# A two-block network on one core: convolution taps handed out step by step, convolution tiles evenly spaced

## The chip, the core and the metric

The kernel runs on one core of one Trainium2 chip. The metric is the device time of one execution in microseconds, the median of a few runs. The engines are TensorE (PE, with PEld for its weight loads), VectorE (DVE), ScalarE (ACT), GpSimd (POOL) and SyncE (SP), which here issues the DMAs. Each works through its own list of instructions in the order in which the program was laid out.

## The reference

Two blocks follow each other, each of two layers, on 512 tokens of width 1024. The first block also carries 256 context tokens through its first layer. Each layer of the first block has a mixer of three branches, and then a feed-forward part:

```
hl, hc = x*(1+scale)+shift, ctx*(1+scale)+shift        # per layer
zl, zc = hl @ w_in + b_in, hc @ w_in + b_in
attn   = softmax(q k^T) v                              # 8 heads, 2 key/value heads, rms norm and rotation on q, k
a, gt  = split(conv columns of z)                      # 1024 channels each
h      = depthwise_conv(a * sigmoid(gt), dw_w, dw_b)   # 31 taps along the tokens, per channel
conv_o = silu(layer_norm(h)) @ pw_w + pw_b
pool_o = (windowed means of 2, 4, 8, 16 tokens, less the token) @ pool_w * pool_scale
m      = gate0*attn + gate1*conv_o + gate2*pool_o
x      = layer_norm(alpha*x + g*(m @ w_out + b_out))
x      = layer_norm(alpha*x + g*ffn(x))                # w_up, a conv of 3 taps, silu, w_down
```

In layer 0 all of this is done for 768 tokens (512 + 256). In layer 1 the context only gives keys and values, and the rest is done for 512 tokens. The second block (latent attention and gated linear attention) isn't touched by the change.

## The kernel before

Activations lie with channels on the partitions, 8 tiles of 128 channels. Weights are loaded by `wload` in pieces of 512 KB; ScalarE rounds a piece to a high part (L183) and VectorE takes the low part (L186). Each projection (`proj`) is three matmuls for each 128 x 128 weight tile.

The mixer of the first block has an attention part and a rest. The attention part is written as eight streams of work, each a Python generator, and `steps[l]` is a string with one letter for each step: k and q are key/value and query projections with norm and rotation, t the transposes of queries, g the first gate's projections, h and i attention heads (one step for 256 query tokens), p the pooling branch with the third gate, c the convolution's input. `mixer` walks through the string and advances the stream of each letter.

A convolution tile takes two c steps in `conv_in`. The first projects 128 channels of `a` and puts them with zero pads into a buffer `gl`. The second projects the gate, multiplies (L591), and then issues the tile's 31 taps: one tensor_scalar (L597) and 30 scalar_tensor_tensor (L599) into a tile `y` (W in the profile), each over 783 columns in layer 0 and 512 in layer 1, each reading what the one before wrote. Then `y` is stored to DRAM (`yd`, L601). All taps of a tile are issued in that one step, at a priority offset of `cprio` = -1500.

What sets the order is a list scheduler: it lays out each engine's instructions by priority among those that it holds to be ready, priority being the place in the program, moved by `high_priority(offset)`. With an offset of -1500 a tap ranks behind what is issued up to 1500 places later.

Softmax of a head (`softmax`): VectorE takes the maximum (L495) and scales it (L497), ScalarE does the exponential (L499), VectorE the reciprocal (L501), ScalarE scales (L502). The probabilities are transposed on TensorE (L533) and split by ScalarE (L299) and VectorE (L300) into T tiles, with which TensorE multiplies the values (pv). L546 and L547 end a head's step.

After the last step comes the rest: the eight `yd` tiles are loaded (L725), column sums on TensorE (st) give mean and variance (`ln`), with L263 subtracting the mean and L738 scaling; meanwhile TensorE does the second gate's eight projections, and then the pointwise projection of the convolution (conv_pw).

Of the kernel before, what the change touches and what calls it, by code (L numbers as in the profile page):

```python
# [15 lines left out]
ALU = mybir.AluOpType  # L16
# [61 lines left out]
class Net:  # L78
# [2 lines left out]
    NC1, NT1, NW1, NU1, NP1, NB1 = 27, 11, 4, 5, 3, 30  # L81
    NC2, NCG, NCM, NG2 = 20, 13, 25, 7
    NWR, NWH = 3, 4
    wprio, cprio = 300, -1500
    wshare_attn, wshare_rest, wshare = 0, 0, 0
    nfirst = (1, 3)
    nrings = (dict(T=12, N="T", Q="T", W=5, U="W", E="X", P="A", KV="A", H="A"),
              dict(T=11, N="T", Q="T", W=4, U=5, E="X", P=3, KV=4, H="A"))
    steps = ("cckkkkggqqqthhhccqqiqiccippppppgtghhhcicqqqiicckkkkpppptppgghhccqqhqcciiippppppggthhchciiipppppp",
             "kkkkqqccggthhccqqiiccppppppggthhccqqiikkkkccppppppggthhccqqiiccppppppggthhcciipppppp")  # L90


    steps2 = "00" + "g0g1g" + "01g0" + "0100" + "cccc" + "1rlm" + "g1g1g1g1" + "v1"
# [478 lines left out]
    def conv_in(self, l, t, hs, segs, yd):  # L572

        nc, tc = self.nc, self.tc
        w = self.wload(self.a["w_in"][l, CH_AG + t], KT, 256)
        n = sum(s[1] for s in segs)
        pa = self.ps("pp")
        self.proj(pa, w, 0, P, hs, segs)
        offs, tot = self.padded(segs, 15)
        gl = self.U()  # L580
        self.zero_pads(gl, segs, offs, tot)
        for o, (c0, sn) in zip(offs, segs):
            nc.scalar.activation(gl[:, o:o + sn], pa[:, c0:c0 + sn], AF.Identity, bias=self.col(l, "b_a")[:, t:t + 1])
        yield
        pg = self.ps("pp")
        self.proj(pg, w, P, 2 * P, hs, segs)
        th = self.al("E")
        nc.scalar.activation(th[:, :n], pg[:, :n], AF.Tanh, bias=self.hbg[:, t:t + 1], scale=0.5)
        for o, (c0, sn) in zip(offs, segs):
            g = gl[:, o:o + sn]  # L590
            nc.vector.scalar_tensor_tensor(g, th[:, c0:c0 + sn], 1.0, g, ALU.add, ALU.mult)  # L591

        with tc.high_priority(offset=self.cprio):
            no = tot - 30
            y = self.al("W")[:, :no]
            ws = self.cw[:, t * 31:(t + 1) * 31]
            nc.vector.tensor_scalar(y, gl[:, 0:no], ws[:, 0:1], self.col(l, "dw_b")[:, t:t + 1], op0=ALU.mult, op1=ALU.add)  # L597
            for i in range(1, 31):
                nc.vector.scalar_tensor_tensor(y, gl[:, i:i + no], ws[:, i:i + 1], y, ALU.mult, ALU.add)  # L599
            for o, (c0, sn) in zip(offs, segs):  # L600
                nc.sync.dma_start(yd[t][:, c0:c0 + sn], y[:, o - 15:o - 15 + sn])  # L601
        yield

    def padded(self, segs, pad):

        offs, o = [], pad
        for _, sn in segs:
            offs.append(o)
            o += sn + pad
        return offs, o  # L610
# [66 lines left out]
    def mixer(self, l, xsrc, hs, toks, region):  # L677

        nc, tc = self.nc, self.tc
        last = l == DEPTH - 1  # L680
        segs = [(0, SEQ)] if last else [(0, SEQ), (SEQ, CTX)]
        ntp = 2 if last else 3
        n = SEQ if last else NTOK
# [7 lines left out]
        yd = [self.dr.tile([P, NTOK], F32, name=self.nm("yd")) for _ in range(KT)]  # L691
# [3 lines left out]
        o = {}  # L695
# [19 lines left out]
            "c": chain(self.conv_in(l, t, hs, segs, yd) for t in range(KT)),  # L715
            "p": chain(self.pool_branch(l, g, hs, segs, o, md) for g in range(4)),
        }
        for step in self.steps[l].replace(" ", ""):
            next(streams[step])
        region(2)  # L720
        self.wshare = self.wshare_rest
        ys = []
        for t in range(KT):
            y = self.B()
# [11 lines left out]
        for t in range(KT):  # L736
            y = ys[t]
# [9 lines left out]
        for pr in range(4):  # L747
            ths = gates[pr]
            w = self.wload(self.a["conv_pw"][l, pr], KT, 256)
            for i in range(2):  # L750
                c = 2 * pr + i
                ps = self.ps("pp")
                self.proj(ps, w, i * P, (i + 1) * P, vs, segs)
                o = self.B()
# [1004 lines left out]
```

## Time and profile before

| what | value |
|---|---|
| median of 3 runs | 3402.8 us (3402.74 to 3403.55) |
| the profiled execution | 3398.06 us, its span 3396.3 us |
| granted TensorE clock, mean of the span | 0.962 |
| PE busy | 3189.1 us, 94% of the span |
| PEld busy | 2663.2 us, 78% |
| DVE busy | 2134.7 us, 63% |
| ACT busy | 1414.4 us, 42% |
| POOL busy | 413.2 us, 12% |

The profile is of one execution. Busy times are sums over the span, which runs through stages with different limits, so the stretches of the two attention parts are read by themselves. Matmuls are pipelined, and a PE that is busy for all of a stretch is not at its peak for that. Behind a wait the profile names the instruction that ended it.

### The profile page before, as it was taken

The numbers are of one execution on the slowest core, as the hardware profiler recorded it, in microseconds if no ns is written. First come the engines' busy times: TensorE is split into PE (matmuls) and PEld (weight loads), VectorE is DVE, ScalarE is ACT, GpSimd is POOL, SyncE is SP. The second block draws the span as 40 slices with busy tenths as digits, with TensorE's granted clock in tenths as the row PEclk, the third lists the DMA queues.
The fourth block names the chain that finished last, engine by engine and source line by source line (L and its number), as shares of the span: only waits on it lengthen the run. The fifth ranks groups of instructions, "written<-read, shape, count | busy, mean of one in ns | idle before, by whom it ended". The sixth has DMA issues, their size and how long they took to land. (4 is left out here: it accounts for less than half of the span.)

```text
span 3396.3 us, 46629 instructions
## 1 busy us (share of the span) xinstructions
PE 3189.1 (94%) x18622; PEld 2663.2 (78%) x18622; DVE 2134.7 (63%) x3158; ACT 1414.4 (42%) x2406; POOL 413.2 (12%) x489
## 2 busy tenths in 40 slices
PE   7999999999999999998999989899998898998898
PEld 4887887878778888887888867888887666996677
DVE  6795968744554444446997966755556655666555
ACT  3444343444432122224444445532346435564464
POOL 2130322201000000002112311000001200122001
PEclk8999998999999999998999999999998998999999
DMA  6232312133333432232222233433243232442323
GB/s 254 70 125 84 122 58 69 60 118 101 100 118 132 141 119 63 60 109 88 72 70 91 78 121 113 150 98 99 88 126 110 88 99 70 156 155 80 99 91 119
DMA packets 112808, 353.45 MB, mean 104 GB/s; under 512 B 13328, under 2 KB 20048, under 8 KB 107472
## 3 DMA queue, kind: packets, MB, share of 16 engines
q1 hardware_dynamic: 112592, 350.48, 32.1%
q8 instruction: 146, 2.39, 0.3%
q14 instruction: 70, 0.57, 0.1%
HBM read 327.10 MB, written 21.23 MB: 103 GB/s over the span
## 5 line engine op out<-in xcount | busy, mean ns | idle before, releaser
L186 DVE TENSOR_TENSOR wl<-wr,wh 128x1024 fp32r<-128x1024 f32 (+1 forms) x482 | 582.7, 1211 | 354.8 <-ACT wh L183 350.2
L183 ACT CAST wh<-wr 128x1024 fp32r<-128x1024 f32 (+1 forms) x482 | 490.8, 1020 | 739.3 <-PE pp L191 692.7
L191 PE MATMUL pp<-A,wh 128*128 128x512 f32 (+1 forms) x3392 | 779.8, 345 | 14.5 <-DVE A L296 5.2
L191 PE MATMUL pp<-C,wh 128*128 128x512 f32 (+1 forms) x2328 | 650.6, 366 | 27.5 <-DVE M L1548 11.0
L191 PEld LDWEIGHTS pp<-A,wh 128*128 128x128 f32 x3392 | 537.1, 190 | 127.3 <-issue 19.7
L191 PEld LDWEIGHTS pp<-C,wh 128*128 128x128 f32 x2328 | 414.8, 192 | 111.3 <-DVE M L1548 12.7
L191 PE MATMUL pp<-A,wl 128*128 128x512 f32 (+1 forms) x1696 | 463.2, 342 | 0.0
L191 PE MATMUL pp<-C,wl 128*128 128x512 f32 (+1 forms) x1164 | 421.3, 363 | 0.0
L191 PE MATMUL pp<-B,wh 128*128 128x512 f32 (+1 forms) x1296 | 316.7, 351 | 0.1
L191 PE MATMUL pp<-M,wh 128*128 128x256 f32 (+1 forms) x1280 | 294.3, 325 | 14.5 <-ACT M L1132 7.1
L191 PEld LDWEIGHTS pp<-A,wl 128*128 128x128 f32 x1696 | 272.6, 190 | 41.5 <-issue 1.9
L599 DVE SCALAR_TENSOR_TENSOR W<-W,cw,W 128x783 f32<-128x783 f32 x240 | 275.5, 1152 | 2.6
L191 PEld LDWEIGHTS pp<-C,wl 128*128 128x128 f32 x1164 | 222.3, 191 | 36.6 <-issue 1.1
L191 PEld LDWEIGHTS pp<-M,wh 128*128 128x128 f32 x1280 | 217.2, 196 | 42.4 <-issue 10.4
L191 PEld LDWEIGHTS pp<-B,wh 128*128 128x128 f32 x1296 | 212.3, 188 | 38.4 <-issue 2.1
L211 POOL TENSOR_TENSOR s<-s,nhalf 128x2 f32<-128x2 f32 (+4 forms) x40 | 54.4, 1360 | 1433.7 <-DVE s L277 1416.4
L191 PE MATMUL pp<-M,wl 128*128 128x256 f32 (+1 forms) x640 | 204.8, 321 | 0.0
L599 DVE SCALAR_TENSOR_TENSOR W<-U,cw,W 128x512 f32<-128x512 f32 x240 | 192.8, 804 | 3.5
L191 PE MATMUL pp<-B,wl 128*128 128x512 f32 (+1 forms) x648 | 194.0, 351 | 0.0
L886 DVE SCALAR_TENSOR_TENSOR B<-pp,cols,B 128x511 f32<-128x511 f32 x66 | 43.4, 658 | 214.7 <-ACT B L883 214.7
L851 DVE SCALAR_TENSOR_TENSOR X<-pp,g,X 128x512 f32<-128x512 f32 (+1 forms) x128 | 77.0, 631 | 146.9 <-PE pp L191 146.6
L883 ACT ACTIVATE B<-pp,cols 128x768 f32<-128x768 f32 (+1 forms) x44 | 38.9, 885 | 231.0 <-PE pp L191 231.0
(402 smaller groups left out, 4753.8 us busy)
## 6 DMA issues: line engine op xcount, KB each, us to landing
wr<-w_in SPq DMA_DIRECT2D x184, 512.0 KB, 3.8
wr<-w_up SPq DMA_DIRECT2D x96, 512.0 KB, 3.8
wa<-w_ada SPq DMA_DIRECT2D x40, 1024.0 KB, 5.0
wr<-w_out SPq DMA_DIRECT2D x64, 512.0 KB, 3.9
wr<-w_down SPq DMA_DIRECT2D x48, 512.0 KB, 3.6
wr<-w_ple_gate SPq DMA_DIRECT2D x32, 512.0 KB, 3.9
Z<-w_ada SPq DMA_DIRECT2D x16, 512.0 KB, 8.4
wr<-conv_pw SPq DMA_DIRECT2D x16, 512.0 KB, 3.8
```

Of the source, the lines that this page charges most:

```text
L183: nc.scalar.copy(hi[:, :n], raw[:, :n])
L186: eng.tensor_tensor(lo[:, :n], raw[:, :n], hi[:, :n].bitcast(F32), ALU.subtract)
L191: return self.nc.tensor.matmul(out, l, r, start=start, stop=stop)
L211: self.nc.gpsimd.tensor_tensor(y, x, self.nhalf[:, :n], ALU.pow)
L599: nc.vector.scalar_tensor_tensor(y, gl[:, i:i + no], ws[:, i:i + 1], y, ALU.mult, ALU.add)
L851: nc.vector.scalar_tensor_tensor(xs[t][:, c0:c0 + sn], ps[:, c0:c0 + sn], g5[:, t, q:q + 1], xs[t][:, c0:c0 + sn], ALU.mult, ALU.add)
L883: nc.scalar.activation(y[:, :n], pa[:, :n], AF.Identity, bias=self.col(l, "fdw_b")[:, f:f + 1], scale=cw[:, 1:2])
L886: nc.vector.scalar_tensor_tensor(y[:, c0 + 1:e], pa[:, c0:e - 1], cw[:, 0:1], y[:, c0 + 1:e], ALU.mult, ALU.add)
```

## The change

Three things change in the first block. The string `steps` of each layer has its c pairs at other places; the order of all other letters stays. Pairs then start every 12 steps in layer 0 and every 9 or 10 in layer 1, where they started 6 to 17 steps apart. `conv_in` no longer issues its taps but puts them into a list, and `mixer` issues some of them after each step, so many that the list is empty when the next pair begins: 2 to 4 a step. And `cprio` is 0, so that a tap ranks by its place in the program. The store of a tile is issued with its last tap.

```
-    wprio, cprio = 300, -1500
+    wprio, cprio = 300, 0
-    steps = ("cckkkkggqqqthhhccqqiqiccippppppgtghhhcicqqqiicckkkkpppptppgghhccqqhqcciiippppppggthhchciiipppppp",
-             "kkkkqqccggthhccqqiiccppppppggthhccqqiikkkkccppppppggthhccqqiiccppppppggthhcciipppppp")
+    steps = ("cckkkkggqqqtcchhhqqiqiipccpppppgtghhcchiqqqiikkkcckpppptppggcchhqqhqiiipccpppppggthhcchiiipppppp",
+             "kkkkqqccggthhqqiccippppppgccgthhqqiicckkkkpppccpppggthhccqqiippppccppggthhiccipppppp")
...
+        self.taps += [(tap, i) for i in range(31)]
         yield
+
+    def some_taps(self, n):
+
+        with self.tc.high_priority(offset=self.cprio):
+            for tap, i in self.taps[:n]:
+                tap(i)
+        del self.taps[:n]
...
-        for step in self.steps[l].replace(" ", ""):
+
+        steps = self.steps[l]
+        cs = [i for i, x in enumerate(steps) if x == "c"]
+        starts = cs[0::2] + [len(steps)]
+        self.taps = []
+        for i, step in enumerate(steps):
+            if i in starts:
+                self.some_taps(len(self.taps))
             next(streams[step])
+            if self.taps:
+                left = min(x for x in starts if x > i) - i
+                self.some_taps(-(-len(self.taps) // left))
+        self.some_taps(len(self.taps))
```

Three places in the resulting order. The first is VectorE's list in layer 0 at the end of the second convolution tile (its `y` is W_1427 before and W_1216 in the change); W_1956 is the third tile's `y`. s are softmax scalars, T probabilities or normed queries, wl the low parts of weights. Before:

```order
L591 SCALAR_TENSOR_TENSOR W_1897<-X_1952,W_1897 128x256
L300 TENSOR_TENSOR T_1787<-pt_1781,T_1786 128x512
L501 RECIPROCAL s_2001<-s_1999 128x1
L599 SCALAR_TENSOR_TENSOR W_1427<-W_1368,cw_310,W_1427 128x783
L597 TENSOR_SCALAR W_1956<-W_1897,cw_310,cols_88 128x783
L599 SCALAR_TENSOR_TENSOR W_1427<-W_1368,cw_310,W_1427 128x783
L495 TENSOR_REDUCE s_2009<-ps_2004 128x1
L599 SCALAR_TENSOR_TENSOR W_1956<-W_1897,cw_310,W_1956 128x783
L497 TENSOR_TENSOR s_2011<-s_2009,s_1085 128x1
```

The change, where taps have the line numbers 599 (the first) and 601:

```order
L601 SCALAR_TENSOR_TENSOR W_1216<-W_1157,cw_310,W_1216 128x783
L186 TENSOR_TENSOR wl_1970<-wr_1968,wh_1969 128x1024
L601 SCALAR_TENSOR_TENSOR W_1216<-W_1157,cw_310,W_1216 128x783
L186 TENSOR_TENSOR wl_1976<-wr_1974,wh_1975 128x1024
L495 TENSOR_REDUCE s_1745<-ps_1737 128x1
L497 TENSOR_TENSOR s_1747<-s_1745,s_1081 128x1
L300 TENSOR_TENSOR T_1633<-pt_1627,T_1632 128x512
L501 RECIPROCAL s_1751<-s_1749 128x1
L300 TENSOR_TENSOR T_1648<-pt_1642,T_1647 128x512
L495 TENSOR_REDUCE s_1762<-ps_1754 128x1
```

Before, the third tile's first tap stands between the second tile's last two; in the change 28 other instructions stand between the two tiles.

The second place is VectorE's list at the end of layer 1's attention part. W_16889 (before) and W_16972 (the change) are the last tile's `y`; L670 and L682 are the same line of the pooling branch. Before:

```order
L300 TENSOR_TENSOR T_17046<-pt_17040,T_17045 128x512
L599 SCALAR_TENSOR_TENSOR W_16889<-U_16857,cw_13005,W_16889 128x512
L300 TENSOR_TENSOR T_17061<-pt_17055,T_17060 128x512
L599 SCALAR_TENSOR_TENSOR W_16889<-U_16857,cw_13005,W_16889 128x512 x3
L300 TENSOR_TENSOR T_17076<-pt_17070,T_17075 128x512
L599 SCALAR_TENSOR_TENSOR W_16889<-U_16857,cw_13005,W_16889 128x512 x2
L547 SCALAR_TENSOR_TENSOR X_16922<-X_16630,X_16922 128x256
L599 SCALAR_TENSOR_TENSOR W_16889<-U_16857,cw_13005,W_16889 128x512 x6
L186 TENSOR_TENSOR wl_17497<-wr_17495,wh_17496 128x1024
```

The change:

```order
L300 TENSOR_TENSOR T_17018<-pt_17012,T_17017 128x512
L300 TENSOR_TENSOR T_17033<-pt_17027,T_17032 128x512
L601 SCALAR_TENSOR_TENSOR W_16972<-U_16940,cw_13005,W_16972 128x512 x3
L300 TENSOR_TENSOR T_17048<-pt_17042,T_17047 128x512
L601 SCALAR_TENSOR_TENSOR W_16972<-U_16940,cw_13005,W_16972 128x512 x3
L547 SCALAR_TENSOR_TENSOR X_16816<-X_16614,X_16816 128x256
L601 SCALAR_TENSOR_TENSOR W_16972<-U_16940,cw_13005,W_16972 128x512 x10
L186 TENSOR_TENSOR wl_17497<-wr_17495,wh_17496 128x1024
L601 SCALAR_TENSOR_TENSOR W_16972<-U_16940,cw_13005,W_16972 128x512 x2
L186 TENSOR_TENSOR wl_17503<-wr_17501,wh_17502 128x1024
L601 SCALAR_TENSOR_TENSOR W_16972<-U_16940,cw_13005,W_16972 128x512 x7
```

The last tile starts later among the heads: behind the last head's L547 stand 19 taps and two weight splits, where 6 taps stood.

The third place is TensorE's list just behind, around the broadcast of the convolution's mean (cmean). pp_17507 and pp_17534 are gate projections, st the sums of the layer norm. Before:

```order
L191 MATMUL pp_17507<-C_12918,wh_17496 128x512
L191 MATMUL pp_17507<-C_12919,wh_17496 128x512
L191 MATMUL st_17312<-B_17310,cmean 128x512
L191 MATMUL pp_17507<-C_12918,wl_17497 128x512
L191 MATMUL pp_17507<-C_12924,wh_17502 128x512
L191 MATMUL pp_17507<-C_12925,wh_17502 128x512
```

The change:

```order
L191 MATMUL pp_17534<-C_12943,wh_17502 128x512
L191 MATMUL pp_17534<-C_12942,wl_17503 128x512
L191 MATMUL st_17312<-B_17310,cmean 128x512
L191 MATMUL st_17322<-B_17326,ones 32x512
L191 MATMUL st_17322<-B_17323,ones 32x512
L191 MATMUL st_17322<-B_17324,ones 32x512
```

Before, 34 gate matmuls stand between the broadcast and the second column sum (st_17322); in the change they have moved ahead of the broadcast.

## Rows read from the trace of the kernel before

**Rows 1.** The page's first part: busy time, share of the span, instructions.

```profile
PE 3189.1 (94%) x18622; PEld 2663.2 (78%) x18622; DVE 2134.7 (63%) x3158; ACT 1414.4 (42%) x2406; POOL 413.2 (12%) x489
```

**Rows 2.** Busy time by stretch of the two attention parts; columns in the first line.

```profile
core 0: us, PE busy (x) PEld busy (x) DVE busy (x) ACT busy (x) POOL busy (x), PEclk, DMA share, GB/s
...
140.00:170.00 30.00, 25.01 (x185) 22.57 (x185) 22.16 (x39) 14.49 (x31) 0.00 (x0) 1.00 0.06 18
170.00:250.00 80.00, 79.32 (x499) 66.41 (x498) 79.57 (x98) 35.02 (x70) 24.11 (x27) 1.00 0.36 115
295.00:325.00 30.00, 24.08 (x166) 19.76 (x164) 16.55 (x39) 19.62 (x42) 0.00 (x0) 1.00 0.11 36
325.00:426.00 101.00, 97.20 (x650) 83.49 (x649) 99.85 (x118) 34.03 (x79) 39.38 (x46) 1.00 0.36 114
475.00:577.00 102.00, 94.77 (x552) 83.13 (x551) 100.74 (x125) 42.53 (x91) 32.90 (x35) 0.92 0.16 49
625.00:690.00 65.00, 57.93 (x331) 49.76 (x330) 58.77 (x75) 29.16 (x50) 22.72 (x21) 0.92 0.27 88
...
1700.00:1785.00 85.00, 77.55 (x517) 70.76 (x516) 78.63 (x121) 39.65 (x82) 15.70 (x13) 0.96 0.22 70
...
1960.00:2003.00 43.00, 34.60 (x182) 28.32 (x181) 40.20 (x66) 22.97 (x37) 4.45 (x5) 0.92 0.30 91
```

**Rows 3.** Costliest groups (busy, mean ns, idle before), and tap durations min/median/max.

```profile
L186 DVE TENSOR_TENSOR wl<-wr,wh 128x1024 fp32r<-128x1024 f32 (+1 forms) x482 | 582.7, 1211 | 354.8 <-ACT wh L183 350.2
L599 DVE SCALAR_TENSOR_TENSOR W<-W,cw,W 128x783 f32<-128x783 f32 x240 | 275.5, 1152 | 2.6
...
L599 DVE SCALAR_TENSOR_TENSOR W<-W,cw,W x240: 1007/1032/2610, 68.1 to 671.0; 128x783 f32<-128x783 f32 x120
L599 DVE SCALAR_TENSOR_TENSOR W<-U,cw,W x240: 732/752/1831, 1601.6 to 2003.5; 128x512 f32<-128x512 f32 x120
```

**Rows 4.** Timeline around 551 us: start, duration, instruction, idle before and releaser.

```profile
551.01 0.15 DVE L497 TENSOR_TENSOR s<-s,s 128x1 f32<-128x1 f32 x1
...
551.20 0.56 ACT L499 ACTIVATE A<-ps,s,s 128x256 f32<-128x256 f32 x1 [1.65 <-DVE s L497]
...
552.41 1.01 PE L191 MATMUL pp<-A,wh 128*128 128x512 f32 x2 [2.57 <-ACT A L299]
```

**Rows 5.** Timeline around 1774 us.

```profile
1773.72 1.28 DVE L300 TENSOR_TENSOR T<-pt,T 128x512 fp32r<-128x512 f32 x2
...
1774.46 1.65 PE L191 MATMUL pv<-T,KV 128*128 128x256 f32 x6 [2.80 <-DVE T L300]
```

**Rows 6.** Timelines of VectorE and of GpSimd around 250 us.

```profile
249.80 2.61 DVE L599 SCALAR_TENSOR_TENSOR W<-W,cw,W 128x783 f32<-128x783 f32 x1
...
248.82 2.75 POOL L672 TENSOR_TENSOR X<-X,X 128x768 f32<-128x768 f32 x1 [1.78 <-DVE X L670]
```

**Rows 7.** Timelines of VectorE and TensorE behind layer 1's attention part.

```profile
1998.34 0.43 DVE L547 SCALAR_TENSOR_TENSOR X<-X,X 128x256 f32<-128x256 f32 x1
1998.69 5.60 DVE L599 SCALAR_TENSOR_TENSOR W<-U,cw,W 128x512 f32<-128x512 f32 x6
...
2026.03 4.87 DVE L263 TENSOR_TENSOR B<-B,st 128x512 f32<-128x512 f32 x8 [1.30 <-PE st L191]
...
1997.63 0.62 PE L191 MATMUL pp<-C,wh 128*128 128x512 f32 x2
...
2014.05 1.07 PE L191 MATMUL st<-B,ones 128*32 128x512 f32 x8
...
2024.97 1.02 PE L191 MATMUL st<-B,cmean 128*128 128x512 f32 x2
...
2033.85 1.06 PE L191 MATMUL st<-B,ones 128*32 128x512 f32 x8
...
2044.33 1.06 PE L191 MATMUL st<-ident,s 128*128 128x128 f32 x8
...
2056.95 2.50 PE L191 MATMUL pp<-C,wh 128*128 128x512 f32 x5 [6.18 <-ACT C L299]
```

More of the change, by code (lines that the diff above doesn't have):

```diff
@@ L591, in conv_in, with tap @@
             nc.vector.scalar_tensor_tensor(g, th[:, c0:c0 + sn], 1.0, g, ALU.add, ALU.mult)
[L593 to L598, printed above, removed]
+        no = tot - 30
+        y = self.al("W")[:, :no]
+        ws = self.cw[:, t * 31:(t + 1) * 31]
+        def tap(i):
+            if i == 0:
+                nc.vector.tensor_scalar(y, gl[:, 0:no], ws[:, 0:1], self.col(l, "dw_b")[:, t:t + 1], op0=ALU.mult, op1=ALU.add)
+            else:
                 nc.vector.scalar_tensor_tensor(y, gl[:, i:i + no], ws[:, i:i + 1], y, ALU.mult, ALU.add)
-            for o, (c0, sn) in zip(offs, segs):
-                nc.sync.dma_start(yd[t][:, c0:c0 + sn], y[:, o - 15:o - 15 + sn])
+            if i == 30:
+                for o, (c0, sn) in zip(offs, segs):
+                    nc.sync.dma_start(yd[t][:, c0:c0 + sn], y[:, o - 15:o - 15 + sn])
+        self.taps += [(tap, i) for i in range(31)]
         yield
+    def some_taps(self, n):
[3 more added lines that the diff above has]
+        del self.taps[:n]
     def padded(self, segs, pad):
```

## The prediction

> **What bounds the kernel now.** I read the page's busy times first: TensorE is busy for 94% of the span, VectorE for 63% [rows 1]. The change touches only the two attention parts of the first block (about 50 to 690 us and 1560 to 2003 us), so I cut these into stretches [rows 2]. In the PE column the reader is to see what is missing to the length of each stretch, in the DVE column whether VectorE is full, in the PEclk column the granted share of the 2.4 GHz level (the other level is 1.2 GHz). Idle time below is a stretch's length less its PE busy time; clock lost is the length times what PEclk lacks to 1. Three kinds of stretch show.
>
> Where two convolution tiles follow each other closely, VectorE is full for some 100 us: 99.85 of 101 and 100.74 of 102 us. TensorE idles 3.8 us in the first and 7.2 us in the second, where it also gets a clock of 0.92, so 0.08 x 102 = 8.2 us of full clock are not granted. The fill between 170 and 250 us costs 0.7 us.
>
> Where heads run without taps, VectorE has room (16.55 of 30 us) and TensorE idles all the same, 5.9 and 5.0 us per 30: that is the latency of a softmax.
>
> At the end of each attention part, taps and the last softmaxes share VectorE: 7.1 us idle and 5.2 us of clock in layer 0, 8.4 and 3.4 us in layer 1. The stretch 1700 to 1785 loses 7.5 and 3.4 us.
>
> How a full VectorE reaches TensorE is seen at 551 us [rows 4]: the scaling of a softmax bound (L497, 0.15 us) stands behind a weight split and a tap. ScalarE's exponential waits 1.65 us for it, the cast behind it on ScalarE is late, and TensorE, which needs that cast for a projection, waits 2.57 us. At 1774 us it is direct [rows 5]: VectorE comes to two probability splits (L300) only at 1773.72, and TensorE waits 2.80 us for them.
>
> **The change part by part.** No instruction is added or removed: 496 taps (16 tiles of 31), the same matmuls, the same DMAs. All that changes is order. A tap takes 1.032 us in layer 0 and 0.752 us in layer 1 at the median [rows 3], so a tile is some 32 or 23 us of VectorE. Two edits do the reordering, and I take them together: the scheduler no longer ranks taps below everything for 1500 steps, and the tiles' starts lie 9 to 12 steps apart, where they lay 6 to 17 apart.
>
> Counting in the two orders, layer 0 has today only two tiles (the first and last) that stand alone: the second and third run into each other, as do the fourth and fifth and the sixth and seventh. Afterwards all eight stand alone, with 8 to 30 other VectorE instructions between one tile's last tap and the next one's first. That is what should shorten the fills.
>
> Terms, with half-clock time counted as lost:
> 1. 475 to 577 us: 7.2 + 8.2 = 15.4 us lost today. Bounds 0 (the loss moves along with the taps) and -15.4 (as at 170 to 250, which lost 0.7). I take half, -8, since half of the taps remain in one fill.
> 2. 325 to 426 us: -2 of 3.8, by the same half.
> 3. 295 to 325 us: three head steps run there on end before the next convolution's matmuls; afterwards two. Bounds 0 and -5.9; I take -3.
> 4. 140 to 170 us: convolution matmuls now come before the heads, but taps come among them too. Bounds -5.0 and +5; I take -1.
> 5. 1700 to 1785 us: 10.9 us lost. Taps that stand directly ahead of a probability split fall from 51 to 29 in layer 1. I take -5, bounds 0 and -10.9.
> 6. The end of layer 1, 1960 to 2003 us: 11.8 us lost. Afterwards the last tile's taps stand behind nearly all softmaxes instead of among them. The heads then look like 295 to 325 us, which lost 20% without taps; 20% of 43 us is 8.6, so -3.
> 7. The seam behind it pays. Today six taps follow the last head's product (L547), 5.60 us, then the store, the loads and the first column sum at 2014.05 us [rows 7]. Afterwards 19 taps and two weight splits follow before the last tap is done: 13 x 0.752 + 2 x 1.21 = 12.2 us later [rows 3, 7]. Cover: TensorE has gate projections; 70 matmuls stand today between the last head's product and the column sum, 131 then. Today's 70 take 2014.05 - 1997.63 = 16.4 us, 0.235 each, so 131 take 30.7. The data would be there 0.7 + 0.43 + 14.3 + 2.4 + 9.8 = 27.6 us after the last product, 9.8 being today's way from last tap to column sum. So the later taps are hidden with 3 us to spare; if the cover is gone, each us is paid. But the gate matmuls spent there are missing later. Between the mean's broadcast at 2024.97 and the second column sum at 2033.85, 34 matmuls fill today, none then, and the eight subtractions end at 2026.03 + 4.87 = 2030.9: some 5 us of idle. Before the pointwise projection 12.6 us pass from 2044.33 to 2056.95; 27 matmuls (6.3 us) and the broadcast's 1.1 us leave 5.2 us idle, where 6.18 us were. In all +4. On the SP queue the last tile's store still stands ahead of the eight loads; the last gate and first pointwise weights have moved ahead of it, so its being late holds no weights back.
> 8. New waits among heads: taps directly ahead of a softmax's reciprocal (L501) rise from 21 to 31 in layer 0. Ten more taps are at most 10.3 us, and most meet an exponential that is still running; +4, bounds 0 and 10.
> The end of layer 0 (12.3 us lost) keeps its order nearly, and its gate projections stand as they did: 0, with bounds of 3 either way.
>
> Sum: -8 - 2 - 3 - 1 - 5 - 3 + 4 + 4 = **-14 us**. The profiled execution took 3398.1 us (1.8 around its span); less 14 is 3384.1. The three runs' median lies 4.7 above it, so 3388.8, say **3389 us**.
>
> A tap stretches when GpSimd works: 2.61 us beside an addition of 2.75 us [rows 6]. Layer 0's 240 taps take 275.5 us where 240 x 1.032 would be 247.7, so 27.8 us are stretch [rows 3]. The head stretches at 140 and 295 us, which get taps now, show no GpSimd work [rows 2]. The Trainium skill, Perfetto Trace Analysis, section Optimizing Scalar/DVE Operations, says that GpSimd's only SBUF port is one that VectorE shares. The trace agrees (2.61 against 1.032 us). By that rule taps should lie where GpSimd is idle, and half of the 27.8 us would leave VectorE's fills; by the trace that is up to 14 us of VectorE's time, of which I count none, since taps also stay beside the query and pool steps.
>
> **The rivals.** *The fills' loss goes whole.* For it: 170 to 250 us is full for 80 us and costs 0.7 us, so losses come late in a fill, and a shorter one may end before. Against: the lone last tile lost 12.3 us in 65. Terms 1, 2 and 5 would take their full 15.4, 3.8 and 10.9, terms 3, 4 and 6 as above 7, and the seam's 4 and half of term 8 come on top: -31, 3372 us.
>
> *No net change.* The scheduler already put taps into what it held to be idle VectorE time, and still does; the same work then causes the same waits elsewhere. For it: most waits are of 1 us, one tap long, and the taps stay between the same softmax links. 3403 us.
>
> *Slower, by lone tiles among heads.* Afterwards the second, fourth and sixth tile of layer 0 each share VectorE with 36 to 40 other instructions, mostly softmax. Today's lone last tile shares with 31 and costs 12.3 us. Three such cost 36.9; the five stretches that they replace cost 5.0 + 0.7 + 5.9 + 3.8 + 15.4 = 30.8. With the seam's 4 us, and layer 1 gaining nothing, that is +10: 3413 us. It decides from 30.8 / 3 = 10.3 us per tile on. Against it: at 170 us such a fill was cheap.
>
> **How the numbers follow.** Forecast 0.40, whole gain 0.15, no net change 0.23, slower 0.22. A measurement tells some 0.2%, 6.8 us, from no change. Faster by more: all of the forecast but its upper edge, and the whole gain, 0.54. Within: 0.24. Slower: the third rival, 0.22. The range runs from just under the whole gain, 3370, to the slower rival, 3413; some 2 in 10 lie outside. The forecast alone would be 3380 to 3397.
>
> **What would show it.** In the profile after, stretches of full VectorE in layer 0 should be 50 to 60 us long and not 100, and the granted clock should not fall to 0.92 over the fill that ends before 577 us today (terms 1, 2). Taps' maximum and sum show the GpSimd part. Term 5 is right if no wait of 2 to 3 us on L300 is left in layer 1. Term 7 shows as idle time of TensorE between the mean's broadcast and the second column sum, about 5 us, which does not exist today. If the first column sum waits for a load, the cover was too short. The prediction is wrong if TensorE's idle time over the six stretches of layer 0, 29.7 us today, stays what it is (no net change), or if a half-clock stretch appears in each of the tiles among heads (slower).

## The result, and the profile after

The changed kernel takes 3426.45 us at the median (3420.51 to 3426.95, four runs), the one before on the same chip 3402.77 (3402.37 to 3403.55). The ratio is 1.0070 (95%: 1.0057 to 1.0082): slower by 23.7 us. The forecast was 3389 us, in a range of 3370 to 3413. The profiled execution took 3426.95 us (span 3424.8, granted clock 0.956; before 3396.3 and 0.962).

The page's first part, answering [rows 1], in the same columns: every engine has as many instructions as before, and busy times differ by less than 1%, apart from GpSimd's (403.0 for 413.2). TensorE's grows by 18.5 us.

```profile
PE 3207.6 (94%) x18622; PEld 2674.8 (78%) x18622; DVE 2136.5 (62%) x3158; ACT 1417.5 (41%) x2406; POOL 403.0 (12%) x489
```

The stretches, answering [rows 2]: after each stretch its length, busy time and count by engine, then granted clock, DMA share and GB/s.

```profile
core 0: us, PE busy (x) PEld busy (x) DVE busy (x) ACT busy (x) POOL busy (x), PEclk, DMA share, GB/s
147.00:177.00 30.00, 21.89 (x117) 18.28 (x116) 27.78 (x44) 13.21 (x25) 0.00 (x0) 0.77 0.00 1
177.00:257.00 80.00, 79.26 (x497) 67.20 (x498) 61.63 (x82) 37.06 (x78) 18.57 (x26) 1.00 0.31 97
330.00:380.00 50.00, 44.16 (x297) 39.48 (x298) 41.42 (x56) 20.53 (x60) 14.65 (x15) 0.86 0.27 85
380.00:485.00 105.00, 104.54 (x629) 89.22 (x627) 70.34 (x88) 32.83 (x53) 23.27 (x32) 1.00 0.34 106
485.00:525.00 40.00, 33.50 (x195) 29.82 (x193) 37.55 (x52) 19.03 (x51) 8.10 (x7) 0.79 0.05 14
525.00:592.00 67.00, 66.37 (x403) 58.66 (x402) 53.82 (x67) 29.64 (x48) 20.07 (x28) 1.00 0.22 64
642.00:710.00 68.00, 56.63 (x311) 47.45 (x310) 62.71 (x82) 28.94 (x52) 20.67 (x21) 0.90 0.24 80
1722.00:1808.00 86.00, 80.04 (x519) 71.54 (x518) 79.15 (x120) 41.14 (x85) 14.05 (x13) 0.98 0.24 72
1980.00:2025.00 45.00, 36.04 (x187) 30.02 (x187) 34.57 (x56) 23.41 (x38) 3.46 (x2) 0.92 0.32 93
```

Loss is again idle time plus length times what PEclk lacks to 1. Three short stretches stand out, those of layer 0's second, fourth and sixth tile: 8.1 + 0.23 x 30 = 15.0 us, 5.8 + 7.0 = 12.8 and 6.5 + 8.4 = 14.9. The end of layer 0 (642 to 710) loses 11.4 + 6.8 = 18.2, where it lost 12.3. The long fill before 577 us, which lost 15.4, is gone as a stretch (525 to 592: 0.6).

Stretches of two kernels don't hold quite the same work, so the two traces are also laid over each other by work done: at a moment of the kernel before, how much later has the changed kernel done the same amount of matmuls (each counted with its usual duration)? Such lags are good to some 2 us. The changed kernel falls behind by 10 us at the second tile; by 10 at the fourth, of which 3 come back; by 13 at the sixth, which all come back in the rest of the fill behind it; and by 7 at layer 0's end. It is some 23 us behind at 700. Layer 1 gives 2 back, and the seam behind it takes 10.

Inside such a stretch, the timeline around 160 us (start, duration, engine, line, instruction, idle before and releaser; "..." stands for lines left out):

```profile
157.17 0.68 DVE L300 TENSOR_TENSOR T<-pt,T 128x512 fp32r<-128x512 f32 x1
157.91 0.85 PE L191 MATMUL pv<-T,A 128*128 128x256 f32 x5 [1.12 <-DVE T L300]
...
159.58 1.03 DVE L601 SCALAR_TENSOR_TENSOR W<-W,cw,W 128x783 f32<-128x783 f32 x1
...
160.53 0.15 DVE L497 TENSOR_TENSOR s<-s,s 128x1 f32<-128x1 f32 x1
160.71 0.99 ACT L499 ACTIVATE A<-ps,s,s 128x768 f32<-128x768 f32 x1 [0.89 <-DVE s L497]
...
161.34 1.44 PE L191 MATMUL pv<-T,A 128*128 128x256 f32 x5 [1.07 <-DVE T L300]
...
171.28 1.43 PE L191 MATMUL pv<-T,A 128*128 128x256 f32 x5 [1.23 <-DVE T L300]
```

One tap of 1.03 us stands ahead of most links of the softmax (a link is an operation that the next engine of the chain waits for: L497, L501, L300); TensorE, which has only heads here, waits about 1 us again and again. No single wait is long, yet the granted clock is 0.77 over the stretch, part of it at the lower level.

The taps' groups, answering [rows 3] (duration min/median/max in ns):

```profile
L601 DVE SCALAR_TENSOR_TENSOR W<-W,cw,W x240: 1010/1034/2614, 68.4 to 694.7; 128x783 f32<-128x783 f32 x120
L601 DVE SCALAR_TENSOR_TENSOR W<-U,cw,W x240: 731/752/1811, 1623.1 to 2036.2; 128x512 f32<-128x512 f32 x120
```

### The profile page after: what moved, and what is told of

Read it like the earlier page. It is cut to its first block, busy times and chain, and to the rows that moved or that the text cites. A ratio compares the mean times of both kernels' runs of the same rounds, so it can differ in the third digit from the quotient of the medians.

```text
span 3424.8 us, 46635 instructions
## 1 busy us (share of the span) xinstructions
PE 3207.6 (94%) x18622; PEld 2674.8 (78%) x18622; DVE 2136.5 (62%) x3158; ACT 1417.5 (41%) x2406; POOL 403.0 (12%) x489
## 5 line engine op out<-in xcount | busy, mean ns | idle before, releaser
L183 ACT CAST wh<-wr 128x1024 fp32r<-128x1024 f32 x482 | 490.2, 1019 | 776.1 <-PE pp L191 723.8
L186 DVE TENSOR_TENSOR wl<-wr,wh 128x1024 fp32r<-128x1024 f32 x482 | 581.5, 1209 | 363.0 <-ACT wh L183 349.7
L601 DVE SCALAR_TENSOR_TENSOR W<-W,cw,W 128x783 f32<-128x783 f32 x240 | 276.9, 1154 | 3.1
L191 PEld LDWEIGHTS pp<-M,wh 128*128 128x128 f32 x1280 | 218.2, 197 | 42.1 <-issue 10.9
```

The source lines that it names most:

```text
L183: nc.scalar.copy(hi[:, :n], raw[:, :n])
L186: eng.tensor_tensor(lo[:, :n], raw[:, :n], hi[:, :n].bitcast(F32), ALU.subtract)
L191: return self.nc.tensor.matmul(out, l, r, start=start, stop=stop)
```

## The experiments

Each run is compared with the kernel before on its own chip. The scatter of one kernel's runs is some 10 us, so ratios and their 95% intervals are used; 0.1% is 3.4 us.

### Which half of the change, which layer

The kernel before with the new rows of steps alone:

```
-    steps = ("cckkkkggqqqthhhccqqiqiccippppppgtghhhcicqqqiicckkkkpppptppgghhccqqhqcciiippppppggthhchciiipppppp",
-             "kkkkqqccggthhccqqiiccppppppggthhccqqiikkkkccppppppggthhccqqiiccppppppggthhcciipppppp")
+    steps = ("cckkkkggqqqtcchhhqqiqiipccpppppgtghhcchiqqqiikkkcckpppptppggcchhqqhqiiipccpppppggthhcchiiipppppp",
+             "kkkkqqccggthhqqiccippppppgccgthhqqiicckkkkpppccpppggthhccqqiippppccppggthhiccipppppp")
```

> The kernel before with nothing but the two new rows of steps; the taps are still handed out in one piece and still rank 1500 steps behind everything. Theory (the places of the tiles are the whole change): 3426 us, as the changed kernel. Rival (handing the taps out in small groups with rank 0 puts them ahead of the softmax links and costs the time): 3403 us, as before.

Measured: 1.0070 (1.0050 to 1.0089), the changed kernel's own ratio.

The opposite, the changed kernel with the old rows:

> The changed kernel with the two old rows of steps, so that only the handing out of taps in groups and the rank of 0 are left of the change. Theory (the places of the tiles are the whole change): 3403 us, within 4 us of before. Rival (handing out and rank cost the time): 3426 us.

Measured: 0.9997 (0.9983 to 1.0010). Handing the taps out in groups, and their rank, do nothing that can be measured here (between 6 us less and 3 more); the places of the `c` steps are the change.

The changed kernel with the old row in layer 1, then with the old row in layer 0:

> The changed kernel with the old row of steps in layer 1 and the new one in layer 0. By cumulative matmul work the changed kernel is some 23 us behind at 700 us, 3 us of which layer 1's attention gives back, and 9 us are lost at the seam behind layer 1. Theory (layer 0's tiles among heads cost most): 3403 + 23 = 3426 us less the scatter of a profile, 3420 to 3427, so that layer 0 alone makes two thirds or more of the loss. Rival (the loss is the seam's, and layer 0's 23 us in one profile are chance): 3403 to 3410 us.

> The changed kernel with the old row of steps in layer 0 and the new one in layer 1. Theory: the seam's 9 us less 3 us in layer 1's attention, 3403 + 6 = 3409 us, with 3403 to 3413 as bounds. Rival (the loss is the seam's): 3412 to 3426 us.

Measured: 1.0063 (1.0043 to 1.0083) and 1.0011 (1.0001 to 1.0020). Layer 0 makes some 21 us, layer 1 and its seam some 4, with an interval that nearly reaches nothing.

### Taps or projections

The changed kernel without most taps of the three tiles (87 of 93 are left out, so the network's result is no longer computed and only the time is of use), and the kernel before without the same ones; these two are called "few taps":

```
-        self.taps += [(tap, i) for i in range(31)]
+        few = l == 0 and t in (1, 3, 5)
+        self.taps += [(tap, i) for i in ((0, 30) if few else range(31))]
...
-            for i in range(1, 31):
+            for i in ((30,) if l == 0 and t in (1, 3, 5) else range(1, 31)):
```

> The changed kernel, but layer 0's second, fourth and sixth tile have only taps 0 and 30 of their 31 (87 taps are left out); everything else stands where the change put it. Theory (taps between the links of the softmaxes cost TensorE the time): the stretches of these three tiles lose 15.0, 12.8 and 14.9 us in the changed kernel (idle and half clock); without the taps they lose about what heads without taps lose, 5 to 6 us each, so that this kernel comes 24 to 30 us below the changed one, 3395 to 3402 us, and within 10 us of the kernel before with the same taps left out. Rival (the tiles' projections, which filled TensorE between the heads, now stand ahead of them, and that costs the time): the losses stay, the time is 3418 to 3426 us, and some 23 us lie between the two kernels with fewer taps.

> The kernel before, with the same 87 taps of layer 0's second, fourth and sixth tile left out, as the yardstick for the changed kernel without them. The long fills of 325 to 426 and 475 to 577 us lose 3.8 and 15.4 us; with the taps of one tile of two gone, 10 to 19 us of these should go: 3384 to 3393 us by the theory that full VectorE costs the time. By the rival (filler decides) nothing goes: 3400 us.

Measured: 0.9993 (0.9982 to 1.0004) and 0.9957 (0.9941 to 0.9973). The same 87 taps cost 0.77% = 26 us where the change puts them and 0.43% = 15 us where they were. 0.36% = 12 us still lie between the two without them, so these taps are not all. By work done the two differ by only 2 us over the three pairs of tiles (140 to 590 us), where the full kernels differ by 16; what is left lies at layer 0's end and at the seam, some 8 us each, less 2 in layer 1 (the table further down). So the places of these 87 taps account for nearly all that layer 0 loses before its end, and for nothing of its end.

How a link of the softmax stands without taps ahead, in the timeline of the changed kernel with few taps:

```profile
157.24 0.17 DVE L501 RECIPROCAL s<-s 128x1 f32<-128x1 f32 x1 [1.21 <-ACT A L499]
...
158.46 0.86 PE L191 MATMUL pv<-T,A 128*128 128x256 f32 x5 [0.34 <-DVE T L300]
```

VectorE waits for ScalarE here, not the other way round, and TensorE's wait here is 0.34 us, where it was 1.12.

The tiles behind their heads. The edit moves three pairs; the sixth tile's too, which the expectation doesn't name:

```
-"cckkkkggqqqtcchhhqqiqiipccpppppgtghhcchiqqqiikkkcckpppptppggcchhqqhqiiipccpppppggthhcchiiipppppp"
+"cckkkkggqqqthhhccqqiqiipccpppppgtghhhcciqqqiikkkcckpppptppgghhccqqhqiiipccpppppggthhcchiiipppppp"
```

> The changed kernel with one edit to layer 0's row of steps: the two steps of the second tile stand behind the three head steps instead of ahead of them, the fourth tile's behind one head step more. The tiles stay alone. Theory (a tile whose taps meet heads without projections costs 13 to 15 us): the second tile's loss of 15.0 us falls to 5 to 6 and its taps move to the query and key projections behind, so 3415 to 3418 us; the fourth tile, whose taps still meet the same softmaxes, keeps its loss. Rival (lone tiles cost the time wherever they stand): 3426 us.

Measured: 1.0028 (1.0017 to 1.0040), 0.42% = 14 us below the changed kernel. In the trace the second tile's loss goes, the sixth falls, the fourth stays, as was said:

```profile
140.00:170.00 30.00, 24.99 (x186) 22.56 (x184) 22.01 (x39) 14.34 (x30) 0.00 (x0) 1.00 0.07 18
330.00:380.00 50.00, 47.42 (x320) 41.98 (x321) 33.07 (x44) 19.05 (x64) 21.12 (x24) 0.89 0.38 124
485.00:525.00 40.00, 36.51 (x230) 31.71 (x229) 39.54 (x46) 16.77 (x48) 21.49 (x20) 1.00 0.10 26
```

(At the fourth tile 8.1 us are seen in this stretch; by work done it is 11 behind there, of which 3 come back.) The sixth tile's stretch at 485 us loses 3.5 us with VectorE just as full as in the changed kernel: a full VectorE does not cost TensorE time by itself.

### Can the fill's gain be had alone

The kernel before with the seventh tile behind the three head steps and the first pooling step that followed it (the expectation calls this one step later):

```
-"...gghhccqqhqcciiippppppggthhchciiipppppp"
+"...gghhccqqhqiiipccpppppggthhchciiipppppp"
```

> The kernel before with one edit to layer 0's row of steps: the two steps of the seventh tile move one step later, behind the pooling step that stood after them, as in the changed kernel; nothing else moves. In the order this parts the sixth and seventh tile, whose 62 taps fill 475 to 577 us and lose 15.4 us there. Theory (the fill's late half is what costs, and the change's gain there can be had alone): 8 to 15 us less than before, 3385 to 3395 us on a chip where before takes 3400. Rival (the loss moves along to where the seventh tile goes): 3400 us.

Measured: 0.9999 (0.9991 to 1.0007): the theory failed. The stretches of this run, whose profiled execution (3408.78 us) is 8 us above its median:

```profile
500.00:552.00 52.00, 48.67 (x291) 42.09 (x290) 45.63 (x60) 25.54 (x49) 14.56 (x18) 1.00 0.18 56
552.00:577.00 25.00, 23.59 (x138) 19.86 (x137) 24.22 (x26) 8.28 (x12) 10.46 (x14) 1.00 0.29 96
645.00:710.00 65.00, 52.91 (x288) 41.92 (x287) 43.80 (x62) 25.61 (x43) 10.53 (x9) 0.87 0.39 140
```

The fill's end is clean (1.4 us lost, clock 1.00), and by work done some 12 us are won there; 4 of them are paid ahead of it, beside the sixth tile, and 10 at layer 0's end (12.1 idle and 8.5 of clock).

Two more places: the seventh tile behind the three head steps but ahead of the pooling steps, and the eighth earlier; then four tiles beside projections:

```
-"cckkkkggqqqthhhccqqiqiccippppppgtghhhcicqqqiicckkkkpppptppgghhccqqhqcciiippppppggthhchciiipppppp"
+"cckkkkggqqqthhhccqqiqiccippppppgtghhhcicqqqiicckkkkpppptppgghhccqqhqiiiccppppppccggthhhiiipppppp"
...
+"cckkkkggqqqthhhccqqiqiccippccppppgtghhhiqccqqiikkcckkpppptppccgghhqqhqiiiccppppppggthhhiiipppppp"
```

> The kernel before with layer 0's seventh tile one step later (as in the run with one pair moved) and its eighth four steps earlier, ahead of the gates instead of between the last heads; layer 1 as before. When the seventh tile alone was moved, the fill before 577 us gave 13.4 us, the stretch at 500 to 547 us took back 5.3 and the end of layer 0 some 10. Theory (the end paid because the eighth tile's taps, starting later, met more of the last heads): with the eighth tile ahead of the heads these lose what heads without taps lose, 20% of 43 us = 8.6 instead of 12.3: 3400 - 13 + 5 - 4 = 3388 us, bounds 3380 to 3394. Rival (the loss moves along wherever the tiles go, since the last heads lack projections, not VectorE): 3397 to 3404 us.

> The kernel before with layer 0's fourth, sixth, seventh and eighth tile set so that their taps run beside query, key and pooling projections and end before the heads that follow; the second and third tile stay, the fifth moves two steps. In the order 54 taps stand directly ahead of a link of a softmax in layer 0, where the kernel before has 69 and the changed one 83. Theory (what a tap costs depends on whether it stands between the links of a softmax): the fill of 475 to 577 us gives most of its 15.4 us back and the last heads some 4, while pooling steps, beside which a tap stretches to 2.6 us, take some 4: 3385 us, bounds 3375 to 3394. Rival (the same losses turn up elsewhere): 3397 to 3406 us.

Measured: 1.0011 (0.9998 to 1.0024) and 1.0005 (0.9995 to 1.0016). Both rivals hold. Where the second run, with fewer taps ahead of links (54), still loses is seen at 320 us and at 360 us, with all instructions first, and then at 320 us with TensorE's on `pp` (the projections) alone:

```profile
320.00:340.00 20.00, 14.58 (x81) 12.19 (x79) 10.45 (x24) 12.31 (x23) 0.00 (x0) 0.86 0.01 4
360.00:380.00 20.00, 15.36 (x116) 13.98 (x115) 19.89 (x23) 4.62 (x15) 5.07 (x3) 0.92 0.29 90
...
320.00:340.00 20.00, 0.00 (x0) 0.86 0.01 4
```

At 320 us no tap is near (VectorE 10.45 of 20), no projection runs, and 5.4 us idle and 2.8 of clock are lost: heads left alone lose by themselves. But at 360 us VectorE is full again (19.89 of 20), taps stand between the last heads' probability splits, TensorE waits up to 1.23 us for one of these, and 4.6 + 1.6 us are lost.

The new row in layer 1 with the last tile's second step where it was:

```
-"...ppccggthhiccipppppp"
+"...ppccggthhcciipppppp"
```

> The kernel before with the new row of steps in layer 1, but its last tile's second step one step earlier, where it was; layer 0 as before. In the order 23 instead of 10 other VectorE instructions stand among the last tile's taps, so it ends nearer to the last head. Theory (layer 1's attention gains 3 us and the seam behind it costs, because the last tile ends late): the seam's cost goes, 3397 us where the new row as it is took 3404. Rival (the last tile's place is not what costs at the seam): 3404 us.

Measured: 1.0005 (0.9994 to 1.0015), which isn't told apart from the 1.0011 of the new row as it is. In its trace the seam costs nothing more (-1 us by work done), but the last heads cost some 3 to 5: paid before instead of behind.

### Query projections among the heads

In the changed kernel no projection runs from 150.5 to 179.9 us, as its timeline shows:

```profile
150.24 0.28 PE L191 MATMUL pp<-wh,A 128*128 128x256 f32 x1
...
178.75 0.68 DVE L394 TENSOR_TENSOR T<-pp,brow 128x512 f32<-128x512 f32 x1
...
179.88 0.28 PE L191 MATMUL pp<-wh,A 128*128 128x256 f32 x1
```

By the code `pp` has two PSUM buffers, and the results of two query projections stand in them until VectorE reads the first (L394, at 178.75 us). That this comes so late because its T buffer is held by the heads is argued from the code and not shown. Setting `q` steps between `h` steps lets them go on, in layer 0's new row (first), in the old (second), and in the old with two tiles moved (third):

```
-"cckkkkggqqqtcchhhqqiqiipccpppppgtghhcchiqqqiikkkcckpppptppggcchhqqhqiiipccpppppggthhcchiiipppppp"
+"cckkkkggqqqtcchqhqhiqiipccpppppgtghqhcchqiqiikkkcckpppptppggcchqhqhqiiipccpppppggthhcchiiipppppp"
...
-"cckkkkggqqqthhhccqqiqiccippppppgtghhhcicqqqiicckkkkpppptppgghhccqqhqcciiippppppggthhchciiipppppp"
+"cckkkkggqqqthqhccqhiqiccippppppgtghqhqhcicqiicckkkkpppptppgghqhccqhqcciiippppppggthhchciiipppppp"
+"cckkkkggqqqthqhccqhiqiccippppppgtghqhqhcicqiicckkkkpppptppgghqhqhqcciiiccppppppggthhchciiipppppp"
```

> The row of layer 0 that the change brings, with the query steps set between the head steps at three places; the convolution's steps stay ahead of the heads; layer 1 as before. In the order 90 taps stand directly ahead of a link of a softmax in layer 0; with the changed kernel's row it is 83. Theory (what costs is that no projection can run among the heads): the three tiles' losses of 15.0, 12.8 and 14.9 us fall to some 5 each, so from the 3421 us that layer 0's new row gave alone to 3393 us, bounds 3385 to 3403. Rival (taps between the links cost): 3421 us or more.

> The kernel before with the query steps of layer 0 set between the head steps at three places; the convolution's steps keep their places among the others, and as many taps as before stand ahead of softmax links (70, before 69). Theory (projections among the heads decide): the head stretches at 140 to 170 us (5.0 us lost), 295 to 325 (5.9) and 540 to 577 (some 14) lose a third of that: 3400 - 17 = 3383 us, bounds 3375 to 3391. Rival (taps decide): 3398 to 3402 us.

> As the run before it (query steps among the heads), and at the third place the sixth tile stands behind the heads h and the seventh behind the heads i, instead of among and ahead of them. Theory (projections among the heads decide; in the order the last heads of layer 0 have more projections among them than before): a further 2 to 6 us less than the run before it, 3379 us, bounds 3370 to 3389. Rival (as for the seventh tile alone: what the fill gives, the end takes): the same as the run before it.

Measured: 1.0054 (1.0040 to 1.0069), 1.0001 (0.9989 to 1.0012) and 1.0022 (1.0013 to 1.0032). The theory that projections alone decide falls: 3 of the 21 us come back in the first by the ratios, nothing in the second, and the third is slower. In the second the first two places do win, some 3 and 5 us by work done, and 8 are paid between 320 and 440 us. One of the waits there, in its timeline:

```profile
414.32 2.33 POOL L645 TENSOR_TENSOR W<-W 128x776 f32<-128x776 f32 x1 [1.31 <-DVE A L300]
415.23 2.25 DVE L599 SCALAR_TENSOR_TENSOR W<-W,cw,W 128x783 f32<-128x783 f32 x1
...
417.40 0.68 DVE L300 TENSOR_TENSOR T<-pt,T 128x512 fp32r<-128x512 f32 x1
...
418.13 0.66 PE L483 MATMUL pt<-ident,T 128*128 128x128 f32 x4 [1.99 <-DVE T L300]
```

A tap stretched to 2.25 us, beside a GpSimd addition of 2.33, holds a split that TensorE waits for. It is the split of transposed queries (L483), not of a softmax: again a tap ahead of a link, in another chain and at a new place.

### The square

Layer 0's new row with few taps, without and with query steps among the heads (the edits of above, together):

> Layer 0's new row of steps on the kernel before, layer 1 as before, with the 87 taps of layer 0's second, fourth and sixth tile left out. Both theories: the changed kernel without these taps took 3401 us, and layer 1's new row costs some 4 of it: 3397 us, bounds 3392 to 3402.

> The same with the query steps set among the head steps at three places, and the same 87 taps left out. If the two causes add up (heads without projections lose time by themselves, taps or not), the query steps take back their 7.7 us here too: 3389 us, bounds 3385 to 3393, which is where the kernel before stands without these taps. If taps cost only where no projection runs and heads lose nothing by themselves that projections can fill, the query steps bring nothing here: 3395 to 3400 us.

Measured: 0.9977 (0.9965 to 0.9989) and 0.9968 (0.9958 to 0.9978). The taps are worth 0.86% = 29 us in both pairs (1.0063 to 0.9977, 1.0054 to 0.9968), about twice what the same taps cost in the old row; the query steps 0.09% = 3 us in both, which the intervals don't tell from nothing.

The second tile's stretch, 140 to 180 us, shows both more sharply, since up to 140 us all kernels run alike (within 2 us by work done). In this order: before; changed; layer 0's new row with q among heads; few taps; few taps and q among heads; before with q among heads.

```profile
140.00:180.00 40.00, 35.01 (x256) 31.11 (x256) 32.16 (x50) 20.23 (x47) 7.86 (x6) 1.00 0.13 40
```

```profile
140.00:180.00 40.00, 31.16 (x187) 27.08 (x186) 37.60 (x59) 16.77 (x32) 0.00 (x0) 0.83 0.04 13
```

```profile
140.00:180.00 40.00, 32.63 (x215) 28.73 (x214) 38.34 (x55) 17.97 (x37) 3.50 (x3) 0.87 0.17 58
```

```profile
140.00:180.00 40.00, 34.55 (x250) 30.19 (x249) 21.92 (x44) 25.19 (x56) 6.01 (x6) 1.00 0.11 39
```

```profile
140.00:180.00 40.00, 36.32 (x261) 32.26 (x261) 21.32 (x40) 22.82 (x51) 5.49 (x6) 1.00 0.19 65
```

```profile
140.00:180.00 40.00, 38.07 (x271) 33.24 (x270) 32.90 (x49) 19.24 (x45) 7.67 (x9) 1.00 0.28 93
```

| loss in 140 to 180 us (idle + clock) | query steps behind the heads | among them |
|---|---|---|
| taps ahead of the heads (new row) | 8.8 + 6.8 = 15.6 | 7.4 + 5.2 = 12.6 |
| the same, few taps | 5.4 | 3.7 |
| taps behind the heads (before) | 5.0 | 1.9 |

Taps in front of heads cost 9 to 10 us in this stretch, projections among the heads give 2 to 3, and the two add up: with projections among the heads, taps in front of them cost about as much as without. In these 40 us 27 and 24 taps start in the dear cases (VectorE busy 37.6 and 38.3), 14 and 13 in the kernels with the old row (32.2 and 32.9), 1 in those with few taps (21.9 and 21.3). So by these rows half a tile, begun behind the first heads, costs nothing over no tile at all, and most of a tile in front of them 9 to 10 us.

## Why the prediction was wrong

**The view of the bound held.** TensorE is lost to links of softmaxes that stand behind taps, as read at 551 us [rows 4] and as the kernels with few taps show.

**The sum, stretch by stretch.** Us lost (+) or won (-) against the kernel before, by work done; "rows" is the kernel before with the new rows of steps alone, "layer 0" the changed kernel with layer 1's old row. Differences of 2 us say nothing, and the two profiled executions lie 28.9 us apart, 5 more than the medians.

| stretch of the kernel before | terms | forecast | changed | rows | layer 0 | changed, few taps | before, few taps |
|---|---|---|---|---|---|---|---|
| 140 to 250 us, second and third tile | 4 | -1 | +10 | +11 | +10 | +1 | -2 |
| 250 to 470, fourth and fifth | 2, 3 | -5 | +7 | +6 | +7 | -1 | -5 |
| 470 to 590, sixth and seventh | 1 | -8 | 0 | 0 | -2 | -9 | -4 |
| 590 to 705, end of layer 0 | | 0 | +7 | +9 | +7 | +8 | 0 |
| 1600 to 1998, layer 1 | 5, 6 | -8 | -2 | -1 | +2 | -3 | 0 |
| 1998 to 2100, seam | 7 | +4 | +10 | +8 | 0 | +8 | 0 |

Term 8's +4 was spread over layer 0's heads.

**The step that failed: terms 1, 3, 4 and 8, what a tile costs when it is set alone among heads.** The prediction took half of the long fill's loss as won (-8) and put the taps that land on heads at almost nothing (-3, -1 and +4 in all). Term 1's loss did not go: the fill's end came clean, and the sixth tile, now in front of its heads at 485 us, loses as much (14.9 for 15.4). That is the bound of 0 that term 1 itself named, "the loss moves along with the taps". Term 4 gave the heads at 140 us -1, bounded by +5; they cost +10. Term 3 counted on -3; the fourth tile there costs +10, of which 3 come back. Term 2's loss did go (380 to 485 us loses 0.5), but what it wins is small beside that. Without the 87 taps the new row loses nothing at these places.

The rows for a lone tile among heads were at hand: the last one, 12.3 us in 65 [rows 2]. The prediction used it for the rival and, for the forecast, set against it that the fill at 170 us cost 0.7. That row was the wrong neighbour: of TensorE's 79.3 busy us there 65.5 are projections, and five softmaxes run in 80 us; from 147 to 177 us of the changed kernel it is 3.5 of 21.9, and five in 30. The stretch at 140 us was also misread as one without taps: the second tile begins in its middle, and 11 taps follow up to 170 us.

```profile
154.82 0.68 DVE L597 TENSOR_SCALAR W<-W,cw,cols 128x783 f32<-128x783 f32 x1
```

**The rival "slower, by lone tiles among heads"** is what happened, with 15.0, 12.8 and 14.9 us for the 12.3 it priced and above its threshold of 10.3, and with the sign that was named for it, a half-clock stretch in each of the three tiles. It had 3413 us, +10. What it lacked up to 3426 is a tile's price (2 us more each), the 6 us that the stretches between the tiles still lose (it put them at nothing), layer 0's end (held at 0 with 3 either way; +7) and the seam; layer 1 gave a little back.

**Term 5** was a gain, by half: its stretch loses 7.7 us instead of 10.9, and the wait at 1774 us [rows 5] is gone, but one of the kind is left among the last heads, against the prediction's own sign:

```profile
2013.28 1.12 PE L191 MATMUL pv<-T,KV 128*128 128x256 f32 x6 [2.16 <-DVE T L300]
```

**Term 6** was to give 3: 1980 to 2025 us loses 9.0 + 3.6 = 12.6, where 11.8 were lost. Nothing.

**Term 7** had its mechanism right and its size wrong. The seam, answering [rows 7], in TensorE's timeline:

```profile
2059.05 1.94 PE L191 MATMUL st<-B,ones 128*32 128x512 f32 x8 [4.37 <-ACT B L242]
2061.44 1.94 PE L191 MATMUL st<-B,ones 128*32 128x512 f32 x8 [0.46 <-ACT B L242]
...
2086.60 2.50 PE L191 MATMUL pp<-C,wh 128*128 128x512 f32 x5 [5.65 <-ACT C L299]
```

The late taps are hidden and the wait ahead of the second column sum is 4.4 us (5 were said). What was left out is the clock: behind that wait the eight sums take 1.94 us where they took 1.06 [rows 7]. From the last head's product to the pointwise projection it is 9.6 us more, not 4. With layer 0 as before the same row made the seam only some 5 us dearer; why is open.

**Two edits taken together.** The prediction did not separate them; the first two runs show that only the new rows of steps do anything that can be measured.

**The stretch beside GpSimd**, counted as none, stayed: the 240 taps of layer 0 take 276.9 us in all and 240 x 1.034 = 248.2 at the median, 28.7 of stretch where it was 27.8. The Trainium skill, Perfetto Trace Analysis, section Optimizing Scalar/DVE Operations, says that GpSimd's only SBUF port is one that it shares with VectorE. The tap of 2.25 us beside GpSimd's addition at 414 us, shown above, agrees with that. Moving the tiles apart did not take taps out of GpSimd's way.

**What stays open.** Why layer 0's end pays: in all nine kernels whose seventh tile stands behind the first pooling step, it costs 7 to 10 us by work done, with the 87 taps or without. Moving the eighth tile ahead, with the seventh ahead of the pooling steps, made it 13. With the seventh there, the eighth as before and query steps among the heads the end cost nothing (-1), but the stretch of the sixth and seventh tile lost 10 instead. What takes back the 8 us that query steps win at two places of the old row is seen in one wait and not counted through. No layout tried beats the kernel before; six lie within 0.2% of it (layer 1's new row, the seventh tile moved, the eighth early, four tiles beside projections, layer 1's last pair, query steps among the heads of the old row).

## What to carry to other kernels

Price a piece of filler from a stretch that has the same neighbours. A full VectorE cost TensorE 0.7 us in 80 where softmaxes were few, and a tile of 32 us cost some 10 us where it stood in front of heads, whether or not query projections ran among them. When a full stretch is split, ask what the parts land on before counting the gain: here the 15 us that the fill gained were lost again by the tile just ahead of it, and two more landing places came on top with 10 and 7. Lay two traces over each other by work done before calling a stretch's loss won; a loss can leave one stretch and stand in the next. Where a change has two edits, find out first whether each of them changes the order at all.

## What was not expected of the hardware

The granted clock fell without any long wait. In the changed kernel it is 0.66 from 160 to 180 us, a mean over both levels (1.2 and 2.4 GHz), where TensorE's waits are 1.2 us at the longest, as they are in the 20 us before:

```profile
160.00:180.00 20.00, 14.83 (x65) 12.16 (x66) 18.47 (x32) 8.95 (x20) 0.00 (x0) 0.66 0.00 1
```

With few taps TensorE idles 3.1 us in the same 20, with some projections among the heads, and the clock stays at 1.00. But the kernel before idles 5.0 us in 20 among its heads at 300 us, in waits of up to 1.2 us, and keeps 1.00 too:

```profile
300.00:320.00 20.00, 14.98 (x95) 11.42 (x95) 12.03 (x27) 13.40 (x26) 0.00 (x0) 1.00 0.16 53
```

So neither the longest wait nor the idle time alone tells from these rows whether the clock falls; why it fell in one and not in the other is not shown. Where it falls, it can nearly double the price of many short waits: of the 42.7 us that the three tiles lose, 22.3 are clock.
